# The context's gates computed by token: 512 columns of weights past 128 standing tokens

## The chip, the cores and the metric

The kernel runs on one core of one Trainium2 chip. The metric is the device time of one execution in microseconds (us). The kernel before took 1831.76 us, the median of three runs (1830.86 to 1832.96).

## The reference, cut to what matters

Two layers of a block with four parallel branches (retention, short convolution, conformer convolution, windowed attention) work on a sequence of 512 tokens and on a context of 256 tokens, model width 1024, each branch 512 wide. The context's own output is needed in layer 0 alone. At the end of each block the branches are gated and summed:

```
def mixer_output(p, ret_o, att_o, ...):
    r, s, f, a = ...                          # four branches, 512 wide each
    gates = jnp.split(p['merge_gates'], N_BRANCH, axis=-1)
    merged = sum(jax.nn.sigmoid(g) * (br @ w_branch[i])
                 for i, (g, br) in enumerate(zip(gates, (r, s, f, a))))
    return merged @ w_out
```

`merge_gates` is the part of `h @ w_in` with 4 x 1024 columns, where `h` is the normed and modulated input (1024 wide). So one branch of the context costs a product of 256 x 1024 by 1024 x 1024 (the gate), one of 256 x 512 by 512 x 1024 (the branch), a sigmoid, a multiplication and an addition.

## The kernel before, in words

Everything is kept transposed: channels on the 128 partitions, tokens along the row. A projection takes a block of 128 x 128 weights as the standing operand and lets the tokens move past it, 512 columns for the sequence (`x0`, `x1`), 256 for the context (`c0`, `c1`). To keep float32 accuracy with TensorE's faster float32 form, each operand is cut into a high and a low part (`split`, L506, for activations; `w_split`, L445, for weights): ScalarE copies the high part, VectorE subtracts it. Each product is then three matmuls: high x high, high x low, low x high (`mm3`).

The order of the work is: `start` (L1346) norms the context; `mixer(c0)` (L1179) runs the context's projections and branches and then its gates; `mix_out(c0)` (L1242) is its output projection; then the same for the sequence, then layer 1.

`gates` (L1134) is called once per branch, in the order short convolution, retention, attention, conformer. It goes over 8 blocks of 128 output channels. For a block it takes the weights (`w_get`, L467), runs 24 matmuls of the gate into one PSUM bank and 12 matmuls of the branch into another, ScalarE takes the tanh, VectorE multiplies `(tanh + 1) * branch`, and from the second branch on adds the result to the sum `st.acc[n]`. Behind block n of the last branch `late` (L1224) cuts the finished sum into its two parts for the output projection. Ahead of a branch's last two blocks `late` drains the flows of the next branch and cuts that branch's four rows into parts.

Weights come by `w_load` (L425, on SP's queue) and are cut by `w_split` into one of three pairs of tiles `wh`, `wl` (L292) of 1024 columns, up to two tiles ahead (`w_ahead`, L461). For the context a tile is loaded and cut in two pieces of 512 columns; a gate block brings a third piece with the branch's weights.

PSUM has three banks `d` for these projections (L302), used in turn, four banks `k` for everything else, and one bank `ov`.

Convolutions, attention, retention, norms and the modulation of the next stream are flows: generators that are stepped by `slot` (L337), as long as a model of the engines' times says that VectorE and ScalarE have not more than a few us ahead of them. `gates` has one such turn for each block. TensorE's instructions keep the order in which they are written, from all of these together (L1505: `manual_schedule` for TensorE); on the other engines the framework orders instructions itself, by its own estimate of when each is ready.

Lines in the trace are all L187, since one helper records every operation; groups are told apart by tile names: `d<-r,wh` and `d<-r,wl` are projections with the weights' parts, `d<-r,r` the branch products, `k` banks the rest, `cst` the constants (the identity for transposes among them).

Of the kernel before, what the change touches and what calls it, by code (L numbers as in the profile page):

```python
# [11 lines left out]
AF = mybir.ActivationFunctionType  # L12
ALU = mybir.AluOpType
# [12 lines left out]
P = 128  # L26
DEPTH = 2
D = 1024
KC = D // P
# [11 lines left out]
O_G = 6912  # L41
# [48 lines left out]
def _consts():  # L90
    c = np.zeros((P, NC_), np.float32)

    def put(n, v):
        o, w = COFF[n]
        c[:, o:o + w] = v
    i = np.arange(P, dtype=np.float32)
    put("ident", np.eye(P))
    put("a1", np.maximum(i[None, :] - i[:, None], 0))
    put("a2", np.maximum(i[:, None] - i[None, :], 0))
    put("rf", np.tile((i + 1)[:, None], (1, 4)))  # L100
    put("rb", np.tile((P - i)[:, None], (1, 4)))
    put("cf", np.tile((P - 1 - i)[:, None], (1, 4)))
    put("cb", np.tile(i[:, None], (1, 4)))
    pos = np.arange(SEQ)
    inv = (np.float32(10000.0) ** (-np.arange(16, dtype=np.float32) / np.float32(16.0))).astype(np.float32)
    ang = np.concatenate([(pos // 64).astype(np.float32)[:, None] * inv[None],
                          (pos % 64).astype(np.float32)[:, None] * inv[None]], axis=-1)
    put("cos", np.tile(np.cos(ang).T, (4, 1)))
    put("sin", np.tile(np.sin(ang).T, (4, 1)))
    put("mprev", np.where(i[None, :] < i[:, None], NEG, 0.0))  # L110
    put("mnext", np.where(i[None, :] > i[:, None], NEG, 0.0))
    put("ones", 1.0)
    put("mean", 1.0 / D)
    put("sel", np.tile(np.eye(2), (P // 2, 1)))
    put("mhalf", -0.5)
    put("e", math.e)
    return c


NROWS = 59  # L120
PAD = 480


class Row:
# [3 lines left out]
    def __init__(self, free, ring, tile, w, parts):  # L128
        self.free, self.ring = free, ring
        self.r = tile[:, :w] if parts else None  # L130
        self.a = tile[:, :w].bitcast(F32) if parts else tile[:, :w]
# [139 lines left out]
def cs(c):  # L271
    return slice(c * P, (c + 1) * P)
# [3 lines left out]


class Block:
    def __init__(self, ctx, tc, xc, vec, cst, w_a, w_g, w_b, w_o, w_m, out, out2):
        self.tc, self.nc = tc, Tally(tc.nc)  # L280
        self.xc, self.out, self.out2 = xc, out, out2
        self.wsrc = {"a": w_a, "g": w_g, "b": w_b, "o": w_o}
        self.w_m = w_m

        rp = ctx.enter_context(tc.tile_pool(name="rp", bufs=1))
        rp.tile([P, PAD], F32, name="fill")
        self.arena = Arena(rp, NROWS, 12)
        self.arena.relief = self.relief

        self.cp = cp = ctx.enter_context(tc.tile_pool(name="cp", bufs=1))  # L290
        self.wraw = [cp.tile([P, 1024], F32, name=f"w{i}") for i in range(2)]
        self.wt = [[cp.tile([P, 1024], F32R, name=f"w{p}{i}") for p in "hl"] for i in range(3)]  # L292
        self.pt = [cp.tile([P, 640], F32, name=f"p{i}") for i in range(6)]
        pp = ctx.enter_context(tc.tile_pool(name="pp", bufs=1, space=PSUM))
        nc = self.nc
        self.cst = cp.tile([P, NC_], F32, name="cst")
        self.vec = cp.tile([P, NV], F32, name="vec")
        nc.sync.dma_start(self.vec, vec)
        nc.sync.dma_start(self.cst[:, :NCE], cst[:, :NCE])
        self.late_consts = lambda: nc.sync.dma_start(self.cst[:, NCE:], cst[:, NCE:])  # L300
        self.rings = {}
        self.dense = [pp.tile([P, 512], F32, name=f"d{i}") for i in range(3)]  # L302
        self.ovs = [pp.tile([P, 512], F32, name="ov")]
        self.work = [pp.tile([P, 512], F32, name=f"k{i}") for i in range(4)]
        self.turn = {}
        self.wq, self.wraws, self.wready, self.wkeep = [], [], {}, {}
        self.lanes = [[] for _ in range(5)]
        self.turns = 0
        self.flow = None
# [824 lines left out]
    def gates(self, st, i, br, late):  # L1134
        nc = self.nc
        t = st.t
        for n in range(KC):
# [15 lines left out]
            del tg  # L1153
            late(n)

    def conv_first(self, st):

        return not st.s and st.l == DEPTH - 1

    def weights_order(self, st):  # L1160
        b = [("ak", 0), ("av", 0), ("ax", 0), ("ay", 0), ("ax", 1), ("ay", 1)]
        a = [(nm, h) for h in range(4) for nm in ("rq", "rk", "rv")] + [("rz", h) for h in range(4)]
        f = [(nm, j) for j in range(4) for nm in ("cg", "ca")]
        s = [(nm, j) for j in range(4) for nm in ("sc", "sx", "sb", "sz")]
        if self.conv_first(st):
            a, f = a[:12] + [x for j in range(4) for x in f[2 * j:2 * j + 2] + a[12 + j:13 + j]], []
        z = [(nm, j) for nm in ("az", "cz") for j in range(4)]
        g = [("g", st.l, i * KC + n, st.s) for i in (1, 0, 3, 2) for n in range(KC)]
        o = [("o", st.l, n, st.s) for n in range(KC)]
        return [("a", st.l, CIDX[x], st.s) for x in (b + f + a + s + z if st.s else b + a + s + f + z)] + g + o  # L1170

# [7 lines left out]
    def mixer(self, st, kvst, after_ret=None, at_gates=None):  # L1179

        t = st.t
        st.acc, st.m = [], []
        r, a, s, f = ([None] * 4 for _ in range(4))
        self.kv_proj(st)
        fa = []
        for g in range(2):
            xy = [self.copy(self.proj(st, (n, g)), t) for n in ("ax", "ay")]
            fa.append(self.spawn(self.attention(st, kvst, g, xy, a), L_ATT))
            del xy
        fr, zr, ys, zs, za, fc = [], [], [None] * 4, [], [], []  # L1190

        def cf(j):
            fc.append(self.spawn(self.cf_conv(st, j, self.cf_glu(st, j), ys), L_CF))

        first = self.conv_first(st)
        if st.s:
            for j in range(4):
                cf(j)
        for h in range(4):
            q = self.copy(self.proj(st, ("rq", h)), t)  # L1200
            k, v = self.ret_kv_proj(st, h)
            fr.append(self.spawn(self.retention(st, h, k, v, q, zr, r), L_RET2 if st.s and h % 2 else L_RET))
            del q, k, v
        for h in range(4):
            if first:
                cf(h)
            zr.append(self.silu2(self.proj(st, ("rz", h)), t))
        for j in range(4):
            s[j] = self.short_conv(st, j)
        if not (st.s or first):  # L1210
            for j in range(4):
                cf(j)
        for n, z in (("az", za), ("cz", zs)):
            for j in range(4):
                z.append(self.silu2(self.proj(st, (n, j)), t))
        fc.append(self.spawn(self.cf_finish(st, ys, zs, f), L_CF))
        fa.append(self.spawn(self.att_finish(st, kvst, a, za), L_ATT))
        del ys, zs, za, z, zr
        br = [self.split(s.pop(0)) for _ in range(4)]
        order = [(1, s, []), (0, r, fr), (3, a, fa), (2, f, fc)]  # L1220
        for x, (i, _, _) in enumerate(order):
            nxt = []

            def late(n):  # L1224
                if x == 1 and n == 0 and at_gates:
                    at_gates()
                if x < 3 and n >= 6:
                    _, b, fl = order[x + 1]
                    if n == 6:
                        self.drain(fl)  # L1230
                        if x == 0 and after_ret:
                            after_ret()
                    for _ in range(2):
                        nxt.append(self.split(b.pop(0)))
                elif x == 3:
                    st.m.append(self.split(st.acc[n], 0.5))
                    st.acc[n] = None
            self.gates(st, i, br, late)
            br = nxt
        st.hx = None  # L1240

    def mix_out(self, st):  # L1242
# [267 lines left out]
```

## Time and profile before

| | |
|---|---|
| median of three runs | 1831.76 us |
| the profiled execution, its own time | 1828.66 us |
| its span, first to last instruction | 1826.9 us |
| TensorE busy | 1798.4 us, 98% of the span |
| VectorE busy | 1326.9 us, 73% |
| ScalarE busy | 851.6 us, 47% |
| mean granted TensorE clock | 0.997 |
| the context's gates | 221.51 to 366.89 us of the span |

Engines are PE (TensorE's matmuls), PEld (its weight loads, beside matmuls), DVE (VectorE), ACT (ScalarE), POOL (GpSimd) and SP (the queue that issues the DMAs). A busy time is the union of an engine's instructions. Matmuls are pipelined: an instruction of 0.28 us can start 0.12 us after the one before it, so the price of one is the distance from start to start. In the windows the four branches of the context follow one another; a busy time stands before the count of its instructions in brackets.

### The profile page before, as it was taken

Reading aid. Unit: us, or ns where it says so; the run is one execution under the profiler, and the core shown is the slowest. Engines: PE = TensorE matmul, PEld = TensorE weight load, DVE = VectorE, ACT = ScalarE, POOL = GpSimd, SP = SyncE. Lnnn points to the kernel's source line nnn. Section 1 sums busy time; section 2 is a strip of 40 time slices with the busy share of each in tenths; the row PEclk is TensorE's granted clock in tenths of the full one; section 3 lists DMA queues with packets and bytes.
Section 4 is the critical chain, followed back from the end, with each engine's and each line's share of the span. In section 5 each row is a group of like instructions: output and inputs, shape, how many; then the busy total and the mean of one; then the engine's idle time right before and its main releaser. Section 6 shows DMA issues by size and latency. Waiting matters only on the chain. (4 is left out here: it accounts for less than half of the span.)

```text
span 1826.9 us, 27582 instructions
## 1 busy us (share of the span) xinstructions
PE 1798.4 (98%) x10242; PEld 1562.3 (86%) x10242; DVE 1326.9 (73%) x2635; ACT 851.6 (47%) x1625; POOL 27.9 (2%) x34
## 2 busy tenths in 40 slices
PE   6999999999999999999999999999999999999998
PEld 4999999988888888888888889888888888888888
DVE  8899999884556669996998457447999866344445
ACT  6666765553554544423423246445534554323223
POOL 1000000000000000000000000000000000000000
PEclk9999999999999999999999999999999999999999
DMA  9646477743222222233555552322222232332233
GB/s 315 246 129 207 120 239 231 233 138 116 70 70 68 83 81 80 95 113 124 183 167 170 159 190 76 116 70 70 65 92 84 84 95 91 111 105 90 87 116 116
DMA packets 104135, 232.60 MB, mean 127 GB/s; under 512 B 12864, under 2 KB 19776, under 8 KB 104000
## 3 DMA queue, kind: packets, MB, share of 16 engines
q1 hardware_dynamic: 104000, 230.84, 39.1%
q8 instruction: 80, 1.31, 0.3%
q14 instruction: 55, 0.45, 0.1%
HBM read 218.73 MB, written 5.24 MB: 123 GB/s over the span
## 5 line engine op out<-in xcount | busy, mean ns | idle before, releaser
L187 PE MATMUL d<-r,wh 128*128 128x512 f32 (+1 forms) x3136 | 942.8, 383 | 0.3 <-DVE r L187 0.3
L187 PEld LDWEIGHTS d<-r,wh 128*128 128x128 f32 x3136 | 572.7, 188 | 106.2 <-DVE r L187 0.8
L187 PE MATMUL d<-r,wl 128*128 128x512 f32 (+1 forms) x1568 | 597.6, 381 | 0.0
L187 DVE TENSOR_TENSOR wl<-w,wh 128x1024 fp32r<-128x1024 f32 x193 | 235.8, 1222 | 234.7 <-ACT wh L187 228.8
L187 ACT ACTIVATE wh<-w 128x1024 fp32r<-128x1024 f32 x193 | 204.9, 1062 | 412.0 <-PE d L187 354.8
L187 PEld LDWEIGHTS d<-r,wl 128*128 128x128 f32 x1568 | 294.8, 188 | 57.8
L187 ACT ACTIVATE r<-r 128x512 fp32r<-128x512 f32 (+3 forms) x264 | 150.6, 588 | 206.6 <-DVE r L187 93.8
L187 DVE TENSOR_TENSOR r<-r,r 128x512 fp32r<-128x512 f32 (+5 forms) x337 | 207.6, 630 | 33.4 <-ACT r L187 29.5
L187 DVE SCALAR_TENSOR_TENSOR r<-r,h_cfw,r 128x503 f32<-128x503 f32 (+19 forms) x360 | 229.4, 649 | 2.0
L187 PE MATMUL d<-r,r 128*128 128x512 f32 x768 | 184.8, 389 | 0.5 <-DVE r L187 0.5
L187 ACT ACTIVATE wh<-r 128x512 fp32r<-128x512 f32 x208 | 129.2, 630 | 101.7 <-PE d L187 90.0
L187 PEld LDWEIGHTS d<-r,r 128*128 128x128 f32 x768 | 144.1, 188 | 30.8 <-DVE r L187 0.9
L187 DVE TENSOR_TENSOR wl<-r,wh 128x512 fp32r<-128x512 f32 x208 | 140.6, 685 | 18.6 <-ACT wh L187 17.6
L187 DVE SCALAR_TENSOR_TENSOR r<-r,d 128x512 f32<-128x512 f32 (+1 forms) x156 | 92.8, 595 | 55.1 <-PE d L187 32.4
L187 ACT ACTIVATE r<-d 128x512 f32<-128x512 f32 (+2 forms) x234 | 118.5, 507 | 14.1 <-PE d L187 9.5
L187 PE MATMUL k<-r,r 128*128 128x128 f32 (+2 forms) x752 | 112.3, 290 | 2.7 <-ACT p L187 2.6
L187 ACT ACTIVATE r<-k 128x512 fp32r<-128x512 f32 (+4 forms) x162 | 77.0, 523 | 70.2 <-PE k L187 68.7
L187 PEld LDWEIGHTS k<-r,r 128*128 128x128 f32 x752 | 99.5, 191 | 9.0 <-ACT p L187 6.2
L187 ACT ACTIVATE p<-k,s_nm 128x256 f32<-128x256 f32 (+1 forms) x144 | 69.7, 496 | 77.0 <-DVE s_nm L187 76.8
L187 DVE SCALAR_TENSOR_TENSOR r<-r,cs,r 128x256 f32<-128x256 f32 x196 | 83.8, 480 | 1.0 <-DMA r<-w_m 0.4
L187 DVE TENSOR_TENSOR r<-k,r 128x512 fp32r<-128x512 f32 (+2 forms) x88 | 54.5, 653 | 9.2 <-ACT r L187 9.0
L187 ACT ACTIVATE p<-p,s_rc 128x512 f32<-128x512 f32 (+2 forms) x80 | 51.3, 719 | 8.6 <-DVE s_rc L187 8.6
(400 smaller groups left out, 2249.0 us busy)
## 6 DMA issues: line engine op xcount, KB each, us to landing
w<-w_a SPq DMA_DIRECT2D x108, 512.0 KB, 3.5
r<-w_a SPq DMA_DIRECT2D x128, 256.0 KB, 4.8
w<-w_g SPq DMA_DIRECT2D x64, 512.0 KB, 3.5
r<-w_m SPq DMA_DIRECT2D x96, 256.0 KB, 3.8
r<-w_b SPq DMA_DIRECT2D x96, 256.0 KB, 3.3
r<-w_g SPq DMA_DIRECT2D x64, 256.0 KB, 3.7
w<-w_o SPq DMA_DIRECT2D x21, 512.0 KB, 3.5
r<-xc SPq DMA_DIRECT2D x24, 256.0 KB, 3.9
```

Of the source, the lines that this page charges most:

```text
L187: return f(*a, **k)
```

## The change

For the context alone, the gates are computed with tokens on the partitions. The standing operand is a block of 128 tokens (of the input's high or low part, as it stands), and 512 columns of weights move past it. A branch goes in two halves of 512 output channels; a half has four weight tiles for the gate and two for the branch product, each tile of 1024 columns being 2 blocks of the inner width x 512 output channels. Two token blocks share each tile: 12 matmuls per tile. There are two gate accumulators and two product accumulators per half, all from the three `d` banks. The sum `st.acc` is four rows of 128 tokens x 512 channels (half, token block). At the end it must have channels on partitions again: `merged_ctx` transposes two blocks for each 128 channels into a `k` bank and cuts the result into its parts. For the first half this is done within the last branch, ahead of the four gate tiles of the second half; for the second half it is done behind the stage. The weights come from a new array `w_c` with the same numbers in the new order. The arena has 63 rows in place of 59.

```
-NROWS = 59
+NROWS = 63
...
+    def gates_ctx(self, st, i, br, late):
+        nc = self.nc
+        def mm(banks, xs, j, last):
+            hi, lo = self.w_get("c", st, next(tiles))[0]
+            for c, ps in enumerate(banks):
+                for k in (2 * j, 2 * j + 1):
+                    xh, xl = xs[k]
+                    ws = slice(512 * (k % 2), 512 * (k % 2) + 512)
+                    for x, (a, b) in enumerate(((xh, hi), (xh, lo), (xl, hi))):
+                        nc.tensor.matmul(ps, a.r[:, cs(c)], b[:, ws], start=(k == 0 and x == 0),
+                                         stop=(last and k == 2 * j + 1 and x == 2))
+        tiles = iter(range(12 * i, 12 * i + 12))
+        for g in range(2):
+            pgs = [self.take("dense") for _ in range(2)]
+            for j in range(4):
+                self.slot()
+                late(g, j)
+                mm(pgs, st.hx, j, j == 3)
+            tgs = []
+            for pg in pgs:
+                tgs.append(self.row())
+                nc.scalar.activation(tgs[-1].a, pg, AF.Tanh, scale=0.5)
+            pbs = [self.take("dense") for _ in range(2)]
+            for j in range(2):
+                self.slot()
+                mm(pbs, br, j, j == 1)
+            for tg, pb in zip(tgs, pbs):
+                nc.vector.scalar_tensor_tensor(tg.a, tg.a, 1.0, pb, op0=ALU.add, op1=ALU.mult)
+            if len(st.acc) <= 2 * g:
+                st.acc += tgs
+            else:
+                for c, tg in enumerate(tgs):
+                    nc.vector.tensor_tensor(st.acc[2 * g + c].a, st.acc[2 * g + c].a, tg.a, op=ALU.add)
+            del tg, tgs
+    def merged_ctx(self, st, n):
+        nc = self.nc
+        ps = self.bank_now()[:, :st.t]
+        for c in range(2):
+            self.transpose(ps[:, cs(c)], st.acc[2 * (n // 4) + c].a[:, cs(n % 4)])
+        hi, lo = self.pair(st.t)
+        nc.scalar.activation(hi.r, ps, AF.Copy, scale=0.5)
+        nc.vector.scalar_tensor_tensor(lo.r, ps, 0.5, hi.a, op0=ALU.mult, op1=ALU.subtract)
+        st.m.append((hi, lo))
...
+        if st.s:
+            g = [("c", st.l, i * 12 + n, st.s) for i in (1, 0, 3, 2) for n in range(12)]
...
+            def late_ctx(g, j):
+                if (g, j) == (0, 0) and x == 1 and at_gates:
+                    at_gates()
+                if (g, j) == (1, 2) and x < 3:
+                    _, b, fl = order[x + 1]
+                    self.drain(fl)
+                    if x == 0 and after_ret:
+                        after_ret()
+                    nxt.extend(self.split(b.pop(0)) for _ in range(4))
+                if x == 3 and g:
+                    self.merged_ctx(st, j)
-            self.gates(st, i, br, late)
+            if st.s:
+                self.gates_ctx(st, i, br, late_ctx)
+            else:
+                self.gates(st, i, br, late)
             br = nxt
+        if st.s:
+            for n in range(4, KC):
+                self.merged_ctx(st, n)
+            st.acc = None
```

## Rows read from the trace of the kernel before

**Rows 1.** The page: busy times of the engines; granted clock in 40 slices.
```profile
PE 1798.4 (98%) x10242; PEld 1562.3 (86%) x10242; DVE 1326.9 (73%) x2635; ACT 851.6 (47%) x1625; POOL 27.9 (2%) x34
PEclk9999999999999999999999999999999999999999
```
**Rows 2.** Busy time by window: length, PE, PEld, DVE, ACT, POOL; clock, DMA share, GB/s.
```profile
221.51:254.45 32.94, 32.94 (x275) 32.77 (x274) 28.75 (x64) 21.63 (x45) 1.17 (x2) 1.00 0.59 185
254.45:289.01 34.56, 34.56 (x290) 34.56 (x289) 32.63 (x74) 19.50 (x40) 0.00 (x0) 1.00 0.81 265
289.83:328.50 38.67, 38.67 (x325) 38.67 (x325) 37.22 (x88) 18.38 (x37) 0.00 (x0) 1.00 0.70 224
330.55:366.89 36.34, 36.34 (x307) 36.34 (x305) 29.13 (x61) 20.56 (x44) 1.12 (x1) 1.00 0.74 247
```
**Rows 3.** TensorE in order of time (start, duration, names): context's gates, a flow's sums.
```profile
330.55 0.28 PE L187 MATMUL d<-r51h,wh 128*128 128x256 f32 x1
...
333.43 0.28 PE L187 MATMUL d<-r564h,r 128*128 128x256 f32 x1
...
334.88 0.95 PE L187 MATMUL k<-cst,r 128*128 128x1 f32 x8
```
**Rows 4.** TensorE in order of time, the sequence's gates, transposes of a flow behind them.
```profile
843.20 0.84 PE L187 MATMUL d<-r,r 128*128 128x512 f32 x3
843.88 0.62 PE L187 MATMUL d<-r,wh 128*128 128x512 f32 x2
...
846.61 1.47 PE L187 MATMUL k<-cst,r 128*128 128x128 f32 x12
847.83 0.71 PE L187 MATMUL d<-r,wh 128*128 128x512 f32 x2
848.38 0.40 PE L187 MATMUL d<-r,wl 128*128 128x512 f32 x1
```
**Rows 5.** TensorE in order of time, two transposes between the context's projections.
```profile
185.02 0.29 PE L187 MATMUL d<-r135h,wl 128*128 128x256 f32 x1
185.15 0.38 PE L187 MATMUL k<-cst,r 128*128 128x128 f32 x2
...
185.60 0.28 PE L187 MATMUL d<-r51h,wl 128*128 128x256 f32 x1
```
**Rows 6.** VectorE in order of time: multiplications, a weight part, a multiplication and addition.
```profile
346.60 0.42 DVE L187 SCALAR_TENSOR_TENSOR r<-r,d 128x256 f32<-128x256 f32 x1
...
367.16 0.42 DVE L187 SCALAR_TENSOR_TENSOR r<-r,d 128x256 f32<-128x256 f32 x1 [0.23 <-PE d L187]
...
376.61 0.68 DVE L187 TENSOR_TENSOR wl<-r,wh 128x512 fp32r<-128x512 f32 x1
...
844.15 0.69 DVE L187 SCALAR_TENSOR_TENSOR r<-r,d 128x512 f32<-128x512 f32 x1 [0.70 <-PE d L187]
844.87 0.69 DVE L187 TENSOR_TENSOR r<-r,r 128x512 f32<-128x512 f32 x1
```
**Rows 7.** TensorE in order of time, the matmuls that belong to the first three.
```profile
344.28 0.28 PE L187 MATMUL d<-r573h,r 128*128 128x256 f32 x1
...
366.77 0.28 PE L187 MATMUL d<-r573h,r 128*128 128x256 f32 x1
...
377.35 0.39 PE L187 MATMUL d<-r580h,wl 128*128 128x256 f32 x1 [0.57 <-DVE wl L187]
```
**Rows 8.** VectorE's groups by form in 221.51 to 366.89: count, busy us, mean ns, idle before.
```profile
L187 DVE SCALAR_TENSOR_TENSOR r<-r,d 128x256 f32<-128x256 f32 x32 | 13.3, 416 | 1.2 <-PE d L187 0.7 <-PE k L187 0.3
...
L187 DVE TENSOR_TENSOR r<-r,r 128x256 f32<-128x256 f32 x23 | 9.6, 419 | 0.1
```
**Rows 9.** TensorE in order of time at the start, its waits in brackets.
```profile
13.33 0.39 PE L187 MATMUL k<-r,s 128*4 128x256 f32 x2 [2.28 <-ACT r L187]
14.84 0.80 PE L187 MATMUL k<-r,s 128*4 128x256 f32 x3 [1.11 <-DVE r L187]
```
**Rows 10.** Busy time by window behind these waits, the granted clock among them.
```profile
14.00:18.00 4.00, 3.16 (x15) 1.59 (x15) 3.83 (x12) 2.50 (x4) 0.00 (x0) 0.57 1.03 392
```

More of the change, by code (lines that the diff above doesn't have):

```diff
@@ L278, with __init__ @@
 class Block:
-    def __init__(self, ctx, tc, xc, vec, cst, w_a, w_g, w_b, w_o, w_m, out, out2):
+    def __init__(self, ctx, tc, xc, vec, cst, w_c, w_a, w_g, w_b, w_o, w_m, out, out2):
         self.tc, self.nc = tc, Tally(tc.nc)
         self.xc, self.out, self.out2 = xc, out, out2
-        self.wsrc = {"a": w_a, "g": w_g, "b": w_b, "o": w_o}
+        self.wsrc = {"c": w_c, "a": w_a, "g": w_g, "b": w_b, "o": w_o}
         self.w_m = w_m
@@ L1483 @@
     w_g = np.stack([blk(A(w_in)[l], np.arange(O_G, O_G + 4096)).reshape(32, P, 1024) for l in range(DEPTH)])
+    w_c = np.stack([np.concatenate([w.reshape(-1, 2, P, 512).transpose(0, 2, 1, 3).reshape(-1, P, 1024)
+                                    for i in range(4) for g in range(2)
+                                    for w in (A(w_in)[0][:, O_G + D * i + 512 * g:O_G + D * i + 512 * g + 512],
+                                              A(w_branch)[0, i][:, 512 * g:512 * g + 512])])])
     w_b = np.stack([np.concatenate([blk(A(w_branch)[l, i], np.arange(D)).reshape(8, P, 512) for i in range(4)])
@@ L1495 @@
                     for l in range(DEPTH)])
-    arrays = {"xc": xc, "vec": vec, "cst": _consts(), "w_a": w_a, "w_g": w_g, "w_b": w_b, "w_o": w_o, "w_m": w_m}
+    arrays = {"xc": xc, "vec": vec, "cst": _consts(), "w_c": w_c, "w_a": w_a, "w_g": w_g, "w_b": w_b, "w_o": w_o, "w_m": w_m}
     arrays = {k: np.ascontiguousarray(v) for k, v in arrays.items()}
```

## The prediction

> **What bounds the kernel now.** I read the page's busy shares first [rows 1]: TensorE is busy for 98% of the span and its granted clock is 1.0 in every slice of it but fractions at the start, so time is gained where TensorE does less or waits less. Then I cut out the stage of the change, the context's four gate branches, with the busy time by window [rows 2]: TensorE is busy for the whole of each window, at clock 1.00, and no wait is left in it. VectorE is close behind, 28.75 of 32.94, 32.63 of 34.56, 37.22 of 38.67 and 29.13 of 36.34 us. ScalarE has 18 to 22 us per branch, and the DMA share is at most 0.81. So the stage is TensorE's, with VectorE as the next to bind.
>
> Then the price of one matmul, by start to start in TensorE's order of time. In the context's gates, 24 matmuls of 256 columns take 333.43 - 330.55 = 2.88 us, 120.0 ns each [rows 3]. In the sequence's gates, where 512 columns move, three take 843.88 - 843.20 = 0.68 us, 226.7 ns each [rows 4]. Two matmuls of 256 columns cost 240.0 ns and one of 512 costs 226.7 ns: 13.3 ns per matmul do not scale with the columns.
>
> **The change, part by part.**
>
> *The matmuls.* Before, the stage has 4 branches of 8 output blocks with 24 + 12 matmuls: 1152 of 256 columns, 1152 x 0.1200 = 138.24 us. After, it has 4 branches x 2 halves x (4 x 12 + 2 x 12) = 576 of 512 columns, 576 x 0.22667 = 130.56 us. That is -7.68 us, all of it on the path, because the stage has no wait that could take it back [rows 2]. Both sides have one weight load per matmul, hidden at these paces. What stands still is now a token block, 128 x 128 as before. I see no bound apart from these rows, and take no spread.
>
> The Trainium skill's page "TensorE: Matmul & The Clock Gate", section "Wait — 56ns, not 53.3ns?", puts the fixed part of a back-to-back matmul at about 2.5 ns. The 13.3 ns of rows 3 and 4 disagree for this data type, and the measurement decides here; by the page the matmuls would give back only 576 x 2.5 ns = 1.4 us, and the sum below would come out near +6 us. That is the last rival below.
>
> *The transposes.* 16 are added. Where a pair stands between matmuls now, 185.02 to 185.60 holds three matmuls of 0.12 and the pair: 0.58 - 0.36 = 0.22 us [rows 5]. Twelve in a row take 847.83 - 846.61 = 1.22 us, 0.102 each, and the two matmuls behind them 848.38 - 847.83 = 0.55 instead of 0.45 us [rows 4]. The first four pairs stand alone among the last branch's matmuls (4 x 0.22 = 0.88), the other four come in a row at its end (8 x 0.102 + 0.10 = 0.91): +1.79 us.
>
> The same page's section "Part 4: PE-mode transpose" gives about 275 ns for a transpose in a kernel's context. The row's 102 ns is start to start and not the duration, so it is what a queue of them costs; by the page's figure the term would be 4.4 us in place of 1.79.
>
> *Two new waits of TensorE.* Its order is the written one. In the last branch the first pair of transposes stands directly behind the last matmul of the first half and reads both sums of that half; the pairs of the second half stand directly behind the stage's last matmul. Each time TensorE must wait until VectorE has multiplied and added, and everything behind (the next gate's 48 matmuls, or the output projection) waits too. Before, the last sum was needed only 21 matmuls (2.5 us) into the output projection. The price from the sequence's gates, where VectorE was free: the last matmul starts at 843.65 (the third of the row at 843.20), the multiplication starts at 844.15 (+0.50), the addition at 844.87, and it ends at 845.56 (+1.91) [rows 4, 6]. From VectorE's end to TensorE's start it is 377.29 to 377.35, 0.06 us [rows 6, 7]. Without the wait the next matmul would start at +0.23. So one wait costs 1.91 + 0.06 - 0.23 = 1.74 us at least. If the first token block's addition comes between, it is 0.72 more, 2.46. I take 2.1. VectorE can also be late: the multiplication that belongs to the matmul at 344.28 began at 346.60, 2.32 after it, against 0.39 at 366.77 to 367.16 [rows 6, 7]; that is 1.93 of backlog, in the very branch where the first wait lies. At the first wait I add 0.6 of it, near the lower end of 0 to 1.93, since the work that fills VectorE there (the next stream's norm) runs only for part of the branch. At the end of the stage the rows show none. Both waits: 2.1 + 0.6 + 2.1 = 4.8 us, bounds 3.5 and 2 x 2.46 + 2 x 1.93 = 8.8.
>
> *Banks.* A half holds two accumulators of the three, so the second gate bank of a half is the first product bank of the half before. From that product's last matmul to the first that overwrites it there are 13 matmuls, 13 x 0.2267 = 2.95 us; VectorE releases it at 0.50 + 0.69 + 0.06 = 1.25, which leaves 1.70 for a backlog. The worst one seen, 1.93, exceeds that by 0.23. There are seven such handovers: 0 to 1.6, I take 0.6, nearer to the rows without backlog.
>
> *VectorE and ScalarE.* Weight splits stay the same: 3 pieces of 512 columns for each of 32 blocks before, 2 for each of 48 tiles after. Multiplications go from 32 x 0.416 to 16 x 0.69 us, additions from 24 x 0.419 (23 of them in the row) to 12 x 0.69 [rows 6, 8]: some 4 us less, off the path. The tanh count halves. The splits of the merged sum read PSUM in place of SBUF, 8 as before. A weight tile now lasts 12 x 0.2267 = 2.72 us for two pieces; the context's projections ran with two pieces in 24 x 0.12 = 2.88 us and VectorE all but full, and TensorE did not wait: no cost, but only 5% from ground that the trace covers. The same bytes come in, in a stage 5% shorter: DMA share some 0.85 at its fullest; SP's queue carries two transfers per tile in place of three per block.
>
> *The output projection's start.* Its first 12 matmuls (1.44 us) need the sums that were split earlier; the last four must be split while the transposes and these run. VectorE has the next stream's modulation in its way (0.6 to 0.7 a piece). I take 0.2, bounds 0 and 1.
>
> **Sum:** -7.68 + 1.79 + 4.8 + 0.6 + 0.2 = -0.3 us. The profiled run took 1828.66 us (span 1826.9 and 1.8 around it), so 1828.4 there; it lies 3.1 under the median of the runs shown, 1831.76, from which the same sum gives 1831.5. Ends: -7.68 + 1.79 + 3.5 = -2.4, and -7.68 + 1.79 + 8.8 + 1.6 + 1 = +5.5.
>
> **Rivals.**
>
> *The waits are covered.* Ahead of each transposed pair of the first half there is a turn in which other flows may put matmuls, and the drain of flows stands behind the second. A small sum of such a flow holds TensorE for some 0.9 us [rows 3]. If both waits shrink to 0.9 us and no bank waits: -7.68 + 1.79 + 1.8 = -4.1, 1827.7. For it: such sums fall into the last branch. Against: they must be due just then, and the second group stands ahead of the drain.
>
> *VectorE binds in the middle branches* (slower). It has 32.63 of 34.56 and 37.22 of 38.67 us there [rows 2]. The matmuls leave each branch 1.92 us less: 32.64 and 36.75. VectorE saves 1.2 us in each (3.3 - 2.8 of multiplying, 3.4 - 2.8 of adding, by the durations above), so it would stand at 31.5 and 36.1: 96% and 98%. From there it decides: if no work can be put off to the last branch (80% busy), both keep their length: -0.3 + 3.84 = +3.5, 1835.3. Against: the modulation sums that fill it are not due before the end.
>
> *The clock falls.* At the start TensorE stood for 2.28 and 1.11 us with two matmuls between, and then the granted clock was 0.57 on the mean over 4 us [rows 9, 10]: one of the two levels, 1.2 GHz, for most of it, 4 x 0.43 = 1.7 us lost. A wait of 2 to 3 us with full work on both sides is milder. One fall gives 1833.2, two 1834.9.
>
> *The fixed part is smaller than the rows say*, so the change does not do what it says: +5.9, 1837.7. Against it stand all rows of either width.
>
> **How the numbers follow.** Forecast 0.50 (its own range 1829 to 1834), covered waits 0.15, VectorE 0.15, clock 0.17, fixed part 0.03. What a measurement can tell from no change is about 0.2%, 3.7 us: below 1828.1 or above 1835.4. Faster: 0.10 from covered waits and 0.04 from the forecast's tail, with the order of flows in the later stages shifted, 0.14. Slower: 0.08 of VectorE, 0.06 of the clock, 0.03, and 0.06 of the forecast's tail, 0.23. The range goes from under the covered case, 1827.0, to 1837.0, above the sum's upper end less the rarest mixes.
>
> **What would show it.** In the changed profile: 512-column matmuls at 226.7 ns in the context's gates and a stage of some 145 us as before; two idle stretches of TensorE of 2 to 3 us ended by VectorE, at the middle and the end of the last branch, directly ahead of transposes. Waits of under 1 us there, or further ones on banks in the first branches, or a granted clock of 0.5 behind one of them, would prove a step wrong; so would VectorE without idle time while TensorE waits for it.

## The result, and the profile after

The changed kernel takes 1846.85 us (median of 4 runs, 1846.25 to 1847.23), the kernel before 1831.85 us (4 runs, 1830.86 to 1832.96). The ratio is 1.0087, 95% interval 1.0075 to 1.0099: 15.0 us, 0.9%, slower. Forecast were 1831.5 us and a range up to 1837.0, so the result is outside it, on the slower side.

The profiled run took 1846.7 us, its span is 1844.6 us, against 1826.9 before; the profile of before was 3.2 us under its median, so the spans differ by 17.7 us where the medians differ by 15.0. The page's busy times of the engines and its row of granted clock in 40 slices, of the changed kernel:

```profile
PE 1802.9 (98%) x9682; PEld 1541.0 (84%) x9682; DVE 1322.5 (72%) x2607; ACT 852.9 (46%) x1609; POOL 28.9 (2%) x34
...
PEclk9999999999999999999999999999999999999999
```

Nothing on this page shows the loss. TensorE has 560 matmuls fewer than in [rows 1], which is 1152 - 576 - 16 as the change says, and is busy for 98% as before; the mean clock of the span is 0.994 where it was 0.997. The place has to be found by time, and first in the stage that was changed. Windows of the changed kernel (length, then busy time of PE, PEld, DVE, ACT, POOL, then granted clock, DMA share, GB/s): the four gate branches; the context's output projection; the attention stage of the sequence in layer 0; the same in layer 1; two short stretches inside these two.

```profile
223.65:368.11 144.46, 141.49 (x657) 116.84 (x655) 131.84 (x267) 87.04 (x156) 2.94 (x3) 1.00 0.70 228
368.11:391.23 23.12, 23.12 (x196) 23.12 (x194) 19.59 (x36) 13.71 (x26) 0.00 (x0) 1.00 0.23 74
694.00:782.00 88.00, 82.16 (x389) 67.36 (x388) 84.37 (x148) 43.05 (x86) 0.00 (x0) 0.98 0.27 88
1390.00:1544.00 154.00, 146.14 (x710) 119.61 (x709) 113.04 (x207) 79.15 (x163) 2.58 (x4) 0.98 0.26 86
...
708.40:711.90 3.50, 3.50 (x14) 2.91 (x13) 3.50 (x8) 0.00 (x0) 0.00 (x0) 0.51 0.39 138
1404.80:1411.60 6.80, 6.44 (x20) 5.14 (x20) 6.02 (x10) 2.79 (x5) 0.00 (x0) 0.50 0.24 77
```

And the first two of these stages in the kernel before, whole:

```profile
221.51:367.35 145.84, 145.84 (x1218) 145.43 (x1216) 129.37 (x289) 82.65 (x168) 2.29 (x3) 1.00 0.71 230
367.35:391.60 24.25, 23.68 (x194) 23.23 (x193) 23.43 (x43) 15.88 (x28) 0.00 (x0) 1.00 0.30 96
```

The changed stage is 1.38 us shorter and the output projection behind it 1.13 us shorter, 2.51 us together. (The window of before ends inside the broadcast of the sequence's norm; with 0.40 us of it that falls behind the border the stage is 1.78 us shorter and the projection 0.73.) They began 2.14 us later (223.65 against 221.51), which comes from the start of the program, where executions of the same instructions differ by 1.7 and 2.6 us (last section), and so the sequence begins at 391.23 and 391.60 us: at this point the change has cost nothing.

Behind it both kernels run the same number of matmuls of 512 columns, so the k-th of them in one trace can be set against the k-th in the other. The changed kernel is 0.37 us ahead at the first, 6.25 us behind from 776 us on, still 6.21 at 1250, and 16.85 us behind from 1530 on: it loses 6.6 us in the attention stage of layer 0, 10.6 us in that of layer 1, and next to nothing between them. No instruction of the diff stands there. TensorE's waits in 391 to 1560 us, grouped by what they wait for (us in total, times, longest), in the changed kernel:

```profile
PE k L187 <- ACT p L187: 14.5, 18, 3.3
PE ov L187 <- DVE r L187: 0.9, 1, 0.9
PE ov L187 <- ACT r L187: 0.6, 1, 0.6
```

and in the kernel before:

```profile
PE k L187 <- ACT p L187: 3.4, 9, 0.7
PE d L187 <- DVE r L187: 0.5, 1, 0.5
PE ov L187 <- DVE r L187: 0.3, 1, 0.3
PE k L187 <- ACT r L187: 0.2, 1, 0.2
```

16.0 us of waits against 4.4: 11.6 us. To these come the two stretches at half clock (the lower of its two levels, 1.2 GHz) in the windows above, 3.5 and 6.8 us at 0.51 and 0.50, in each of which half the work is lost: 5.1 us. Together 16.7 of the 17.2 us. The clock fell where TensorE had just waited: the first stretch follows on the longest wait, the second begins behind one of 2.06 us:

```profile
1404.02 0.33 PE L187 MATMUL k<-cst,p 128*128 128x128 f32 x1 [2.06 <-ACT p L187]
```

The longest wait shows the mechanism. First TensorE in order of time in the changed kernel (start, duration, names, wait in brackets):

```profile
703.96 0.39 PE L187 MATMUL d<-r,wl 128*128 128x512 f32 x1
707.62 0.44 PE L187 MATMUL k<-r,r 128*128 128x384 f32 x1 [3.28 <-ACT p L187]
```

ScalarE in the same stretch of the changed kernel:

```profile
705.43 0.58 ACT L187 ACTIVATE p<-k,s_nm 128x384 f32<-128x384 f32 x1 [2.88 <-DVE s_nm L187]
...
707.00 0.48 ACT L187 ACTIVATE p<-k,s_nm 128x256 f32<-128x256 f32 x1
```

And VectorE there:

```profile
702.38 0.69 DVE L187 TENSOR_REDUCE s_mc<-k 128x2 f32<-128x512 f32 x1
702.99 1.01 DVE L187 TENSOR_REDUCE s_mx<-k 128x1 f32<-128x384 f32 x2
703.92 0.73 DVE L187 SCALAR_TENSOR_TENSOR r<-r,h_cfw,r 128x504 f32<-128x504 f32 x1
704.57 0.15 DVE L187 TENSOR_TENSOR s_mc<-s_mc,s_mx 128x2 f32<-128x2 f32 x1
704.64 0.68 DVE L187 SCALAR_TENSOR_TENSOR r<-r,d 128x512 f32<-128x512 f32 x1
705.24 0.16 DVE L187 SCALAR_TENSOR_TENSOR s_nm<-s_mc,h_nsink 128x2 f32<-128x2 f32 x1
```

TensorE's next instruction is a group of attention scores into a `k` bank that still holds earlier scores. ScalarE must have read them for the exponentials (`p<-k,s_nm`), and these need the negative row maximum `s_nm`. VectorE makes it in four steps (two reductions and two small instructions), and between them it runs a convolution tap (`h_cfw`, 0.73 us) and a gate multiplication (0.68 us): `s_nm` begins at 705.24, four exponentials run one after the other, the last from 707.00 on, and TensorE goes on at 707.62. In the kernel before the same group came 13 us sooner, and waited 0.43 us (TensorE, in order of time):

```profile
694.49 0.44 PE L187 MATMUL k<-r,r 128*128 128x384 f32 x1 [0.43 <-ACT p L187]
```

So the same work stands in another order. The reason is in `slot`: it looks through four lanes of flows (attention, two of retention, and one for norms and modulation) beginning with lane `self.turns % 4`, and through the convolution's lane last; `self.turns` counts the turns since the program's beginning. The new gates have a turn for each of their 48 weight tiles where the old ones had one for each of 32 blocks (+16); the drain behind the gates takes no turn where it took one (-1), that of the sequence's modulated input, behind the output projection, takes four where it took none (+4). At the sequence's first projection the counter stands at 111 in place of 92, that is 3 in place of 0 modulo 4 (the rotation, from here on), and from there on every choice between lanes begins elsewhere. Of TensorE's 7192 matmuls from there to the end of either trace, set side by side by names and widths, some 890 stand in another order, in 48 places.

### The profile page after: what moved, and what is told of

Read it like the earlier page. It is cut to its first block, busy times and chain, and to the rows that moved or that the text cites. A ratio compares the mean times of both kernels' runs of the same rounds, so it can differ in the third digit from the quotient of the medians.

```text
span 1844.6 us, 26364 instructions
## 1 busy us (share of the span) xinstructions
PE 1802.9 (98%) x9682; PEld 1541.0 (84%) x9682; DVE 1322.5 (72%) x2607; ACT 852.9 (46%) x1609; POOL 28.9 (2%) x34
## 5 line engine op out<-in xcount | busy, mean ns | idle before, releaser
L187 DVE SCALAR_TENSOR_TENSOR r<-r,h_cfw,r 128x503 f32<-128x503 f32 (+22 forms) x360 | 229.8, 651 | 2.3
L187 ACT ACTIVATE r<-r 128x512 fp32r<-128x512 f32 (+3 forms) x232 | 131.7, 583 | 205.1 <-DVE r L187 93.3
L187 DVE TENSOR_TENSOR r<-r,r 128x512 fp32r<-128x512 f32 (+4 forms) x293 | 186.1, 645 | 31.3 <-ACT r L187 25.5
L187 ACT ACTIVATE wh<-r 128x512 fp32r<-128x512 f32 x240 | 149.5, 631 | 112.2 <-PE d L187 98.2
L187 DVE TENSOR_TENSOR wl<-r,wh 128x512 fp32r<-128x512 f32 x240 | 162.0, 689 | 18.5 <-ACT wh L187 17.0
L187 ACT ACTIVATE r<-k 128x512 fp32r<-128x512 f32 (+3 forms) x162 | 77.2, 522 | 79.9 <-PE k L187 78.1
L187 PE MATMUL k<-cst,r 128*128 128x128 f32 (+1 forms) x400 | 54.4, 262 | 4.0 <-DVE r L187 3.7
```

The lines of the kernel that those rows point to most:

```text
L187: return f(*a, **k)
```

## The experiments

Each ratio is to runs of the kernel before on the same chip, with its 95% interval.

**1. The changed kernel, the counter set back.** Ahead of the sequence's first mixer:

```
+        self.turns -= 19
         self.mixer(x0, c0, ...)
```

> Edit: the changed kernel, with the counter of turns (which picks the flow that slot steps first) put back by 19 ahead of the sequence's first mixer, to the 92 that it has there in the kernel before. Theory 'turn order': the whole loss lies in the attention stages of the two sequence mixers, because the changed stage has 16 more turns in its gates and 3 more around them, so that the four lanes of flows are served in another rotation (111 mod 4 = 3 in place of 0); with the counter back, the 17.2 us that those stages lose go and the time is 1829 to 1831 us (1846.85 less 17.2). Rival 'the gates themselves' (token blocks standing, other banks, other rows of the arena shift the later stages): no more than 2 us change, 1845 to 1848.

1831.59 us, ratio 1.0006 (0.9997 to 1.0015), 0.6 us above the range expected: 15.3 us under the changed kernel, and level with before, with all of the new gates in it.

**2. The kernel before, with 63 rows and the counter moved on.** The gates stay as they were:

```
-NROWS = 59
+NROWS = 63
...
+        self.turns += 3
         self.mixer(x0, c0, ...)
```

> Edit: the kernel before, its gates untouched, with 63 arena rows (with 59 it finds no free row in that order) and the counter of turns moved on by 3 ahead of the sequence's first mixer, the rotation that the changed kernel has there. Theory 'turn order': it loses in the same two attention stages what the changed kernel loses, 1847 to 1850 us. Rival 'the gates themselves': within 2 us of the kernel before, 1830 to 1834.

1847.81 us, ratio 1.0095 (1.0081 to 1.0109). TensorE's order from there on is that of the changed kernel but for ten small matmuls of a norm, and so, nearly, are the waits (same view and stretch as above):

```profile
PE k L187 <- ACT p L187: 15.1, 19, 3.2
```

The clock is not the same. In this profile it fell in the attention stages for 3.4 us alone (second window below, columns as above), and around the group that had the longest wait in the changed kernel, and waits as long here, it stayed full (first window):

```profile
708.74 0.44 PE L187 MATMUL k<-r,r 128*128 128x384 f32 x1 [3.24 <-ACT p L187]
...
704.00:714.00 10.00, 6.76 (x35) 5.38 (x34) 9.80 (x19) 2.99 (x9) 0.00 (x0) 1.00 0.25 80
1406.90:1410.30 3.40, 3.40 (x12) 2.81 (x11) 3.15 (x6) 1.33 (x3) 0.00 (x0) 0.50 0.25 100
```

So the waits go with the order, and of the 5.1 us of clock only 1.7 us came again. The whole loss is had without the change to the gates, and is gone with the change in place. One edit of a counter carries it.

**3. The kernel before, with 63 rows alone** (the first two lines of the diff above).

> Edit: the kernel before with 63 arena rows in place of 59 and nothing else: the control for the run with the moved counter. Theory 'turn order': 1830 to 1834 us, as before. Rival 'the arena': the four more rows let flows run in another order and cost by themselves 5 us or more, 1837 and up.

1832.51 us, ratio 1.0011 (1.0002 to 1.0020): with four more rows some 220 matmuls of TensorE's order differ from before, in 7 places, and it costs some 2 us. It is a small part of the loss, but not nothing. Experiment 1, which has the new gates with 63 rows and the same rotation, is 0.9 us under this run.

**4. Experiment 1, with the transposes put behind independent matmuls.** Each pair of the first half goes behind the gate tile that follows its sum; the four pairs of the second half go behind the first 12 matmuls of the output projection:

```
                 mm(pgs, st.hx, j, j == 3)
+                if len(st.m) == j and g and done:
+                    self.merged_ctx(st, j)
...
-                if x == 3 and g:
-                    self.merged_ctx(st, j)
...
+            if st.s and n == 0:
+                self.mm3(ps, w, st.m + [None] * 4, ks=range(4))
+                for k in range(4, KC):
+                    self.merged_ctx(st, k)
+                st.acc = None
+                self.mm3(ps, w, st.m, ks=range(4, KC))
```

> Edit: the changed kernel with the counter put back by 19, and with the transposes moved: each pair of the first half behind its gate tile in place of ahead of it, the four pairs of the second half behind the first 12 matmuls of the output projection. Theory: TensorE's two waits for the sum (0.86 us for the norm's broadcast and 1.0 us of wait at the middle of the last branch, 1.8 and 0.5 at its end in the changed kernel's trace) go, and the time is 2 to 3 us under that of the run with the counter alone, 1826 to 1829 us. Rival: the waits only move to the banks or to VectorE, and the time is within 0.7 us of that run.

1828.94 us, ratio 0.9991 (0.9983 to 1.0000), 2.65 us under experiment 1. Between the two profiles the stage and the output projection together go from 169.9 to 166.3 us: TensorE's waits there from 2.9 to 0.6 us, and the clock, which fell behind the second wait in experiment 1, does not fall.

**5. Experiment 1 with 59 rows**: TensorE's order behind the context is that of before but for ten small matmuls of a norm, so what is left is the change itself.

> Edit: the changed kernel with the counter of turns put back by 19 ahead of the sequence's first mixer and with the 59 arena rows of before: from there on TensorE's order is that of the kernel before but for a norm's few small instructions, so what is left of the change is the context's gates alone. Theory 'the gates are worth what their stage shows': the changed kernel's trace has the stage 1.4 us and the output projection up to 1.1 us shorter, and the four more rows cost some 2 us in the last mixer, so 0.5 to 2.5 us under the kernel before. Rival: the same 1 us above it as with 63 rows, the rows having no part in it.

1828.13 us against 1831.38, ratio 0.9986 (0.9977 to 0.9995): 3.25 us faster, more than I expected of it, and more than its profile shows (next section). The waits of the attention stages are those of before to the digit:

```profile
PE k L187 <- ACT p L187: 3.4, 9, 0.7
```

**6. Experiment 5 with the transposes of experiment 4.**

> Edit: as the last, with the transposes moved (each pair of the first half behind its gate tile, the other four behind the first 12 matmuls of the output projection). Theory: the two waits go as they did with 63 rows (2.65 us), 3 to 5 us under the kernel before, the best of all versions. Rival: within 1 us of the kernel before.

1826.55 us, ratio 0.9974 (0.9964 to 0.9985): 4.8 us under before, the best version of these. The end of its stage, TensorE in order of time:

```profile
364.10 0.28 PE L187 MATMUL d<-r548h,wl 128*128 128x256 f32 x1
...
364.92 0.33 PE L187 MATMUL k<-cst,r 128*128 128x128 f32 x1 [0.54 <-DVE r L187]
365.52 0.98 PE L187 MATMUL k<-cst,r 128*128 128x128 f32 x7 [0.27 <-DVE r L187]
...
367.12 0.38 PE L187 MATMUL d<-r565l,wh 128*128 128x256 f32 x1 [0.41 <-DVE r565l L187]
```

With twelve matmuls of the output projection ahead of the transposes, 0.54 us of the wait is left, a wait of 0.41 us for the split sum is new, and the clock does not fall behind them (1.00 in 366 to 370 us).

**7 and 8. The other two starts of the rotation**: experiment 1 with 17 and with 18 in place of 19, which gives rotations 2 and 1.

> Edit: the changed kernel with the counter put back by 17 in place of 19, so that the lanes start in rotation 2 (94 mod 4). Theory 'turn order': the time follows the rotation, whichever way; a number that differs from both 1831.6 (rotation 0) and 1846.9 (rotation 3) by more than 2 us shows that each rotation has its own loss. Rival 'rotation 0 is only the absence of a disturbance': any rotation but 0 costs the same 15 us.

> Edit: the changed kernel with the counter put back by 18, rotation 1 (93 mod 4). Theories as for rotation 2: its own time under 'turn order', some 1847 us under the rival.

1841.03 us, ratio 1.0056 (1.0042 to 1.0069), and 1839.14 us, ratio 1.0043 (1.0031 to 1.0056). With the same 63 rows the rotations 0, 1, 2 and 3 give 1831.6, 1839.1, 1841.0 and 1846.9 us: the time spreads over 15 us with the order alone. So the rival that any rotation but 0 costs the same 15 us falls. The best of the four is the rotation of the kernel before.

**9. The changed kernel with short taps.** TensorE's order stays that of the changed kernel, since the model of the engines still counts the taps at full width; VectorE does them on 64 columns only, which leaves out most of the sequence's convolution:

```
...
+                    nc.add("vector", "scalar_tensor_tensor",
+                           (y.a[:, a:b], u.a[:, a + d:b + d], w(k), y.a[:, a:b]), {})
+                    tap = nc.nc.vector.scalar_tensor_tensor(y.a[:, a:a + 64], u.a[:, a + d:a + d + 64], w(k),
+                                                            y.a[:, a:a + 64], op0=ALU.mult, op1=ALU.add)
```

> Edit: the changed kernel, in which each tap of the sequence's conformer convolution (30 per channel block, 4 blocks, two layers) works on 64 columns in place of some 500, while the planner's model still counts the full width, so that TensorE's written order stays exactly that of the changed kernel. It leaves out most of that convolution. Theory 'attention under the taps': TensorE's waits for the softmax in the two attention stages (14.5 us) come from maxima that stand behind taps on VectorE; with VectorE free there, most of them and the clock falls behind them go, 1828 to 1835 us. Rival 'the order by itself' (too little between two score groups, whatever VectorE does): 1843 us and up.

1827.76 us, ratio 0.9986 (0.9977 to 0.9995), 19.1 us under the changed kernel; the waits for the exponentials shrink from 14.5 to 3.5 us:

```profile
PE k L187 <- ACT p L187: 3.5, 6, 1.3
```

TensorE's matmuls behind the context are in the changed kernel's order, all 7192. VectorE's instructions are not: the framework, which orders them, put some 690 of 1746 elsewhere. So the run shows what relieving VectorE does, by shorter taps and the order that they allow together.

**10. The same cut in the kernel before**, as the control of experiment 9.

> The kernel before, with the taps of the sequence's convolution cut to 64 columns as in the run with short taps of the changed kernel (most of that convolution is left out; TensorE's written order stays that of before). It is the control of that run, which took 1827.8 us, 19 us less than the changed kernel. Theory (the taps cost the changed kernel because its order puts the attention's score groups beside them, while the order of before keeps clear): taking them away here gives little, as the waits of TensorE for ScalarE's exponentials are only 3.4 us in the attention stages: 1826 to 1830. Rival (the taps cost any order as much, so the short run tells nothing of the turn): some 15 us less here as well, 1812 to 1817. Between these, each has a part.

1825.83 us against 1831.17, ratio 0.9973 (0.9964 to 0.9983): 5.3 us. Taking the taps away gives 19.1 us in the changed order and 5.3 us in that of before. So 13.8 us of the taps' price belong to the order, which is nearly all of the 15.0; the rival that the taps cost any order as much falls, though each has a part (1825.83 is 0.2 us under the range expected).

**11. The changed kernel, attention served first in every turn**, whatever the counter says (from the start of the program on, so the context's flows move too):

```
-            lane = self.lanes[(self.turns + i) % n]
+            lane = self.lanes[i]
```

> Edit: the changed kernel with slot always serving the attention's lane first, then the two retention lanes, then the rest, whatever the counter says. Theory 'late attention': the loss of rotation 3 is that attention is served late and meets the convolution's taps, so serving it first always brings 1830 us or less. Rival 'each order has its own pattern': a time of its own between 1831 and 1850, not under rotation 0.

1834.15 us, ratio 1.0021 (1.0011 to 1.0031), with 8.9 us of waits for exponentials where the changed kernel has 14.5:

```profile
PE k L187 <- ACT p L187: 8.9, 14, 1.7
```

Most of the loss goes, but I had put the mechanism as "attention comes late", and by that the time should have been 1830 or less. That form of it falls: serving attention first is no cure, and each order has waits of its own.

## Why the prediction was wrong

*The step that failed* is one that had no term. The sum ended at the output projection's start, as if all behind it kept its order; "the order of flows in the later stages shifted" stands there only as a tail of 0.04, on the faster side. The turns that the change adds should have been counted: one for each weight tile, 48 in place of 32, which `slot` and the rotation in it show. The size could not have been had from the trace of before, but a mechanism of its own, with a chance, could have been given to it: with the same rows the other rotations cost 7.5 to 15.3 us more than rotation 0 (experiments 1, 2, 7 and 8 and the changed kernel). The range was too narrow on the slower side for this, not for a wrong price in the stage.

*In the stage and the output projection* the forecast was -0.3 us and the changed kernel's profile has -2.51, of which the stage has -1.78. The sign is right, the size is off by 2.2 us, by errors that partly cancel: the waits are 1.8 us cheaper, the banks 0.6, the output projection 0.9, and the matmuls give back 1.15 us less.

*The matmuls* are nearly right. Three from the first half of the changed kernel's third branch (TensorE, in order of time):

```profile
300.01 0.39 PE L187 MATMUL d<-wl,r123h 128*128 128x512 f32 x1
300.24 0.39 PE L187 MATMUL d<-wh,r123l 128*128 128x512 f32 x1
300.47 0.39 PE L187 MATMUL d<-wh,r109h 128*128 128x512 f32 x1
```

0.23 us from start to start, the 226.7 ns of [rows 4]. Summed over the stage, the distances behind the gates' matmuls are 138.8 us before and 132.3 after, so 6.5 us came back in place of 7.68: 552 of the 576 take 227.4 ns on the mean, but the 12 that follow other work take 0.32 us each. The rival that the fixed part is smaller is out. *The transposes* are right: 16 before and 32 after take 1.58 and 3.41 us in the stage, 1.83 us more against 1.79.

*The two waits* are where they were put, directly ahead of transposes and ended by VectorE, but cheaper. TensorE in order of time at the middle and at the end of the last branch:

```profile
345.26 0.39 PE L187 MATMUL d<-wh,r495l 128*128 128x512 f32 x1
345.49 1.02 PE L187 MATMUL k<-r,cst 128*128 128x512 f32 x2
346.35 0.27 PE L187 MATMUL k<-cst,r 128*128 128x128 f32 x1
347.64 0.33 PE L187 MATMUL k<-cst,r 128*128 128x128 f32 x1 [1.02 <-DVE r L187]
...
364.71 0.39 PE L187 MATMUL d<-wh,r495l 128*128 128x512 f32 x1
366.77 0.33 PE L187 MATMUL k<-cst,r 128*128 128x128 f32 x1 [1.68 <-DVE r L187]
367.38 0.98 PE L187 MATMUL k<-cst,r 128*128 128x128 f32 x7 [0.27 <-DVE r L187]
```

At the first, two matmuls of another flow (345.49 to 346.35) stand in front, as the rival "the waits are covered" had it, and 1.02 us is left of the forecast 2.7; at the second nothing covers, and 1.68 + 0.27 is close to the 2.1. Together 2.97 in place of 4.8. The second is VectorE's chain of [rows 6], here with a modulation piece (0.75 us) between the two multiplications:

```profile
364.17 0.68 DVE L187 SCALAR_TENSOR_TENSOR r<-r,d 128x512 f32<-128x512 f32 x1
364.77 0.75 DVE L187 SCALAR_TENSOR_TENSOR r<-r,mod,r 128x512 fp32r<-128x512 f32 x1
365.43 0.68 DVE L187 SCALAR_TENSOR_TENSOR r<-r,d 128x512 f32<-128x512 f32 x1
366.03 1.29 DVE L187 TENSOR_TENSOR r<-r,r 128x512 f32<-128x512 f32 x2
```

*Banks*: 0.6 was forecast, and no such wait is there: the three waits of these fences, 2.97 us, are all of TensorE's idle time in the stage (144.46 - 141.49). *VectorE* has 131.84 of 144.46 us and did not bind. With the waits as measured and no banks the sum of the stage would be -2.9, against -1.78 measured; the difference is that of the matmuls, since the other flows put the same 62 matmuls into the stage in both kernels. *The output projection* is 0.73 us shorter where 0.2 more was forecast: before, it had a wait of 0.57 us of its own [rows 7], and in the changed profile it has none.

*The clock*: the row in [rows 1] says only that each slice has 0.9 or more, not 1.0 as the prediction reads it, but the stage's own windows do say 1.00. It fell behind the second wait in experiments 1 and 5 and in three others, but not in the changed kernel's profile nor in experiment 8, all with the same instructions there. Experiment 1 at its end of the stage (TensorE in order of time):

```profile
365.97 0.33 PE L187 MATMUL k<-cst,r 128*128 128x128 f32 x1 [1.64 <-DVE r L187]
...
367.55 0.56 PE L187 MATMUL d<-r537h,wh 128*128 128x256 f32 x1
```

The window behind it, same kernel, with the columns of the windows above (0.57 on the mean, so the lower level for most of it):

```profile
367.00:371.00 4.00, 4.00 (x24) 4.00 (x22) 2.76 (x8) 2.60 (x7) 0.00 (x0) 0.57 0.22 66
```

The output projection took 24.0 to 24.6 us in such profiles and 23.1 without the fall: some 1.3 us, near the 1.7 of the rival. Its chance was put too low: it happened in five of the seven profiles that have this wait.

*The change by itself* is -3.25 us by the medians of experiment 5, with 1.6 us to either side, where -0.3 stood in the forecast, with its end at -2.4. Its traces show less. The stage and the output projection together take 170.1 us in all four profiles with the old gates, and 167.6 to 169.9 in the seven with the new gates and the transposes as in the change, 169.3 in that of experiment 5: 0.2 to 0.9 us less where the clock fell behind the second wait, 1.2 and 2.5 where it did not. Experiments 1 and 3, both with 63 rows, differ by 0.9 us. So the gain is shown, and some 1 us of it has a place; what the rest of the 3.25 is stays open.

What stays open besides is which detail of the order makes one rotation better than another. Experiments 9 and 10 show that the waits for the exponentials go when VectorE is relieved of the taps, and the rows of VectorE above show one place where a tap stands between the steps of a maximum; that this is so at each of the 18 waits isn't shown. Experiment 11 shows that it isn't a matter of serving attention first. Rotation 3 with 59 rows can't be had: in that order the program finds no free row.

## What to carry to other kernels

Where a program interleaves streams by a counter, a budget or a pool of buffers, an edit that adds turns or rows changes the order of everything behind it. Set the instruction order of the untouched stages of both kernels side by side before crediting or blaming the edit; reset the counter behind the edited stage, and judge the edit with the rest of the order held. A transpose that needs a fresh sum is put behind matmuls that need nothing, not in front of them.

## What the runs showed of the hardware that was not expected

Ahead of one group of scores TensorE waited 3.28 us in the changed kernel's profile, and the granted clock was 0.51 over 3.5 us from shortly behind it; ahead of the same group it waited 3.24 us in that of experiment 2, and the clock stayed at 1.00. At the end of the context's gates a wait of 1.64 us in the middle of full work was followed by 0.57 over 4 us in experiment 1, one of 1.68 us at the same instruction by 1.00 in the changed kernel. So the length of a wait alone didn't tell whether the clock fell, and one profile doesn't show what such a wait costs.

The start of the program differs too between executions of the same instructions. TensorE, VectorE and ScalarE run the same instructions up to the context's gates in the changed kernel and in experiments 1 and 8, and these gates began at 223.65, 222.09 and 223.77 us; in the kernel before and in experiment 10 it was 221.51 and 224.15 us. Why isn't shown.
